# Two-layer decoder trunk: one more pair of the second MLP in seven block products, nine landing tiles and four small ones

## The chip, the cores and the metric

The kernel runs on one NeuronCore of one Trainium2 chip. The metric is the device time of one execution in microseconds (us), lower is better; a time given for a kernel is the median of its runs. The core's engines work side by side, each through its own queue in order: PE (TensorE, matmuls), DVE (VectorE), ACT (ScalarE), POOL (GpSimd) and SP (SyncE, which here issues most of the DMAs).

## What is computed

The reference is a trunk of two layers on 256 tokens of width 1024, all in fp32:

```python
for i in range(DEPTH):                     # 2
    mix = moba_attention(h, ...) if i % 2 == 0 else dilated_attention(h, ...)
    h = layer_norm(ALPHA * h + mix, ln_mix_g[i], ln_mix_b[i])
    h = layer_norm(ALPHA * h + sq_relu_mlp(h, mlp_w_in[i], mlp_w_out[i]),
                   ln_mlp_g[i], ln_mlp_b[i])

def sq_relu_mlp(x, w_in, w_out):           # 1024 -> 4096 -> 1024
    return jnp.square(jax.nn.relu(x @ w_in)) @ w_out
```

With 256 tokens the first layer's attention is plain causal attention in 16 heads of 64. The second layer's is dilated attention in 12 heads. The change touches the second layer's MLP alone, the last part of the program, and mostly its product with w_out: 256 tokens by 4096 by 1024.

## The kernel before

Every fp32 product is made of three products of fp32r parts. A tile is split into a rounded part hi and a rest lo (`split`, L414): ACT copies the tile to hi (L416), DVE subtracts hi from it and so makes lo (L421). PE then adds hi·hi, hi·lo and lo·hi in one bank of its accumulator memory (`mm`, L426). One such product of 128 tokens, 128 inputs and 512 outputs is three matmuls of 128x512.

The weights come in fp32 by DMA from SP into landing tiles of 128x1024 (tag raw, NRAW = 8 of them, L62). They are split there into tiles whi (9) and wlo (10).

The product with w_out is cut into 16 pairs, 0 to f. A pair is 256 of the 4096 inputs, two tiles of 128. The letters in `STEPS` (L41 to L44) say how each pair is computed, and in which order. There are two ways:

- **as rows** (letter O, `do_out`, L1298): two weight tiles of 1024 columns are loaded and split (`load_w`, L431), and for each of the two tiles, token halves (m = 0 and 1) and column halves there is one product: eight products, 24 matmuls.
- **as a block product** (letter S, `do_duo`, L1313): the two tiles, two token halves and two column halves form a product of 2x2 blocks, which is made of seven block products (Strassen's scheme in Winograd's form), 21 matmuls (`mm_duo`, L736). It needs sums of blocks on both sides. On the activations' side `duo_sums` (L640) makes four sums on DVE; where both pairs of a chunk are block products (kinds "SS", L660) the fourth sum covers 256 columns, where only one is, 128. On the weights' side `load_left` (L688) loads the first half x of the pair, splits 512 columns of it (tag sc1) and then adds the next columns to it: an accumulating DMA from POOL in two halves (`add_by_dma`, L679, L683). `load_right` (L701) loads the second half y, splits it (1024 columns), splits the summed x (1024), adds x into y and y's halves with two DVE adds of 512 (L782), and splits y again (1024).

Four of the seven products are gathered in four banks of their own (p1, p5, p6, p7) over all pairs. The step z (`combine_alpha`, L1356) combines them on DVE and adds the result to the token rows `tok` together with ALPHA times the residual. What comes after z in the list is "late": its items are rows (`tail`), and `out_and_ln` (L1187) multiplies them for the first 128 tokens, then for the second. The first 128 tokens are then normalised by `ln_half` (L1150), the second by `ln_last` (L1119). The latter divides its 1024 columns into 512 in one bank (left), 256 in another (right), and 256 in an extra bank (`tp`), which comes last.

A LayerNorm on DVE is: BN_STATS over pieces of the row (L1129, L1132, L1159), BN_AGGR (L1099), the power −1/2 on POOL (L1101 or L1106), subtract the mean and scale by g (`stt`, L789, operands mv,g), scale by rstd and add b (L789, operands rstd,b), and store (`store`, L1115).

The results of relu and square pass through tiles ta of 128x512 (`relu_sq`, L1225; NTA = 6, L61), as do the temporary of `combine_alpha` and some of the attention's tiles. `BEHIND_X` (L218) names the pairs whose second split goes into one of the two tiles xs, which hold the MLP's input until its first product is done, instead of whi and wlo.

The order of all work is written out: each operation is recorded by a planner (`Plan`), and the table `ORDER` (L231 on, a list of differences) gives the sequence in which they are issued. Each engine's queue is the part of that sequence that belongs to it, and an instruction that waits holds up those behind it on its engine. `out_and_ln`, `ln_last` and the others fix what depends on what, not the order.

Of the kernel before, what the change touches and what calls it, by code (L numbers as in the profile page):

```python
# [38 lines left out]
HEAD1 = '00'  # L39
STEPS = (  # L40
    "f1 f2 f3:S2:S3 f4:S4:S5 f5:S6:S7 f6:S8:S9 f7:Sa:Sb Sc Sd m g Se z Of O0 O1",  # L41
    "f1 f2 f3:S2:S3 f4:S4:S5 f5:S6:S7 f6:S8:S9 f7:Sa:Sb Sc Sd g Se z Of O0 O1",
)
SQUARES = ("ADDDAAAA", "ADDDAAAA")  # L44
AHEAD_SUM = (True, False)
# [12 lines left out]

OTAGS = {"o": "acc", "p": "tp", "t": "tp"}
HOMES = (("ta", "ta"), ("pt0", "pt1"), ("pt0", "pt1"), ("sc0", "pt1"))  # L60
NTA = 6  # L61
NRAW = 8  # L62
NFIRST = 6
PER = 1024 // (NFIRST * P)

# [4 lines left out]

STAGE_HOME = (("raw", NRAW),) * 4 + (("g", 1), ("b", 1)) + (("tok", 2),) * 2

# [67 lines left out]
class Plan:  # L140
# [74 lines left out]
LEAD = 3  # L215
ADDS = ({2: 0, 3: 0, 5: 0, 7: 0, 9: 0, 11: 0, 13: 0},) * 2
LATE_ENG = "ACT"
BEHIND_X = {12: 0, 13: 1, 14: 0}  # L218
PREPARED = ((("v", 2), ("v", 2), ("g", 1), ("b", 1)), (("ahi", 3), ("alo", 3), ("ahi", 3), ("alo", 3)))
PLANES = ((("sc0", 4), ("sc0", 4)), (("pt0", 2), ("pt1", 2)))  # L220

# [126 lines left out]
)  # L348


# [5 lines left out]
def tile_trunk(  # L356
# [37 lines left out]
    def mk(shape, dt, tag, bufs, space=None):  # L394
        uid[0] += 1
        return plan.buf(Bufs(space or sb, bufs), shape, dt, tag, bufs, f"{tag}_{uid[0]}")
# [7 lines left out]
    def act(n, aps=0, sbuf=False):  # L404
        return n / 1200 + (0.093 if sbuf else 0.055) + 0.093 * aps
# [25 lines left out]
    def load_w(src, n=1024):  # L431
        w = W()
        w.raw = mk([P, 1024], F32, "raw", NRAW)
        w.hi = mk([P, 1024], F32R, "whi", NSLOT["whi"])
# [253 lines left out]
    def load_left(pair, adds):  # L688

        x = mk([P, 1024], F32, "raw", NRAW)  # L690
        hi, lo = [mk([P, 512], F32R, "sc1", 4) for _ in range(2)]
# [9 lines left out]
    def load_right(pair, left, adds, home=None):  # L701

        x, xk, hi, lo = left
        y = mk([P, 1024], F32, "raw", NRAW)
        yk = [(y, 0), (y, 1)]
# [86 lines left out]
    def rotate(xy, ropet):  # L792
# [10 lines left out]
        for half, ps in enumerate(xy):  # L803
            ps = ps()
            b, a = mk([P, 512], F32, "ta", NTA), mk([P, 512], F32, "ta", NTA)
            src = ps
# [168 lines left out]
    def copy_out(n, ps, tag):  # L975
        t = mk([P, 512], F32, tag, NTA if tag == "ta" else 2)
        op("ACT", act(n), lambda: nc.scalar.activation(t.t[:, :n], ps.t[:, :n], AF.Copy), [ps], [t])
        return t
# [16 lines left out]
    def home(tag):  # L995
        return mk([P, 512], F32, tag, {"ta": NTA, "sc0": 4}.get(tag, 2))

# [227 lines left out]
    def relu_sq(ps, eng):  # L1225
        r = mk([P, 512], F32, "ta", NTA)
        op("ACT", act(512), lambda: nc.scalar.activation(r.t, ps.t, AF.Relu), [ps], [r])  # L1227
        if eng == "A":
            op("ACT", act(512, 0, True), lambda: nc.scalar.activation(r.t, r.t, AF.Square), [r], [r])
        else:  # L1230
            tt(512, lambda: r.t, lambda: r.t, lambda: r.t, ALU.mult, [r], [r])
        return r
# [11 lines left out]
    class Mlp:  # L1244
# [17 lines left out]
        def rest(self, between):  # L1262
# [50 lines left out]
            def do_duo(p):  # L1313
# [6 lines left out]
                for k, n in enumerate(duos[at:]):  # L1320
                    if n not in lefts and k <= LEAD:
                        begin(n)
                    if n == p:
                        w1, w2, w3, w4, w5, w6, w7 = load_right(wout[i][p], lefts[p], ADDS[i].get(p, 1), BEHIND_X.get(p))
                a11, a12, a22, s1, s2, s3, s4 = do_pair(p)
# [16 lines left out]
            def combine():  # L1342
                p1, p5, p6, p7 = prods
                z0, z1 = xtok
                t = mk([P, 512], F32, "ta", NTA)
                w = lambda x: (lambda: x.t)
# [9 lines left out]
            def combine_alpha():  # L1356
                p1, p5, p6, p7 = prods
                z0, z1 = xtok
                t = mk([P, 512], F32, "ta", NTA)
                w = lambda x: (lambda: x.t)  # L1360
# [354 lines left out]
```

## Time and profile before

| | us |
|---|---|
| three runs | 536.36, 536.97, 537.08 |
| median | 536.97 |
| the profiled execution, own time | 535.33 |
| its span in the profile | 533.5 |
| around the span | 1.83 |

| engine | busy us | share of the span |
|---|---|---|
| PE, matmuls | 525.0 | 98% |
| PEld, weight loads beside them | 435.6 | 82% |
| DVE | 502.3 | 94% |
| ACT | 426.9 | 80% |
| POOL | 28.8 | 5% |

The profile is one execution. Times are counted from the start of the span. In a timeline each line gives the start, the duration, engine, line of the kernel, operation, output <- inputs by the program's names, shapes and how many equal instructions were joined; in brackets stand the idle time just before it and what ended that. Durations on DVE and ACT overlap the next instruction's start a little, and matmuls overlap much, so the price of one in a row is the distance of two starts. In the windows the number in brackets behind a busy time is the number of instructions, and PEclk is the clock that TensorE was granted, 1.00 being full speed. The LayerNorm behind the second attention stands at 361 us; everything behind that is the second MLP, and the last matmul ends at 526.6.

### The profile page before, as it was taken

The numbers are of one execution on the slowest core, as the hardware profiler recorded it, in microseconds if no ns is written. First come the engines' busy times: TensorE is split into PE (matmuls) and PEld (weight loads), VectorE is DVE, ScalarE is ACT, GpSimd is POOL, SyncE is SP. The second block draws the span as 40 slices with busy tenths as digits, with TensorE's granted clock in tenths as the row PEclk, the third lists the DMA queues.
The fourth block names the chain that finished last, engine by engine and source line by source line (L and its number), as shares of the span: only waits on it lengthen the run. The fifth ranks groups of instructions, "written<-read, shape, count | busy, mean of one in ns | idle before, by whom it ended". The sixth has DMA issues, their size and how long they took to land. (4 is left out here: it accounts for less than half of the span.)

```text
span 533.5 us, 8128 instructions
## 1 busy us (share of the span) xinstructions
PE 525.0 (98%) x2867; PEld 435.6 (82%) x2868; DVE 502.3 (94%) x801; ACT 426.9 (80%) x608; POOL 28.8 (5%) x39
## 2 busy tenths in 40 slices
PE   9999999999999999999999999999999999999994
PEld 7988888788888888887878888888888887888784
DVE  6899996998999999999999999989889999999997
ACT  6589999548999998998645579846899998999740
POOL 0000000000010111011010000001001110110101
PEclk9999999999999999999999999999999999999998
DMA  8995788539899989989965748555888898999822
GB/s 332 390 406 146 173 288 217 198 112 242 301 211 248 260 226 313 247 197 233 349 242 191 266 169 194 173 187 127 268 237 218 226 303 219 279 273 201 250 82 79
DMA packets 79721, 123.68 MB, mean 232 GB/s; under 512 B 51264, under 2 KB 52160, under 8 KB 79680
## 3 DMA queue, kind: packets, MB, share of 16 engines
q1 hardware_dynamic: 76320, 113.26, 69.3%
q0 software_dynamic: 1920, 6.29, 7.6%
q10 hardware_dynamic: 1440, 3.61, 2.1%
q8 instruction: 22, 0.36, 0.3%
q14 instruction: 19, 0.16, 0.1%
HBM read 110.30 MB, written 1.05 MB: 209 GB/s over the span
## 5 line engine op out<-in xcount | busy, mean ns | idle before, releaser
L421 DVE TENSOR_TENSOR wlo<-raw,whi 128x1024 fp32r<-128x1024 f32 (+2 forms) x206 | 240.6, 1192 | 10.6 <-ACT whi L416 10.0
L416 ACT ACTIVATE whi<-raw 128x1024 fp32r<-128x1024 f32 (+2 forms) x204 | 206.1, 1038 | 38.2 <-PE acc L426 10.3
L426 PE MATMUL acc<-whi,xs 128*128 128x512 f32 (+1 forms) x400 | 118.7, 383 | 0.3 <-ACT ta L1227 0.2
L426 PEld LDWEIGHTS acc<-whi,xs 128*128 128x128 f32 x400 | 73.5, 188 | 15.6 <-ACT ta L1227 0.8
L426 PE MATMUL tp<-whi,xs 128*128 128x512 f32 x240 | 70.8, 393 | 0.0
L426 PE MATMUL acc<-xs,whi 128*128 128x512 f32 (+1 forms) x272 | 67.1, 358 | 0.0
L426 PE MATMUL acc<-wlo,xs 128*128 128x512 f32 (+1 forms) x200 | 66.0, 381 | 0.0
L426 PE MATMUL acc<-whi,ahi 128*128 128x512 f32 (+1 forms) x146 | 57.2, 392 | 0.0
L426 PE MATMUL acc<-wlo,ahi 128*128 128x512 f32 (+1 forms) x146 | 56.4, 386 | 0.0
L426 PE MATMUL acc<-whi,alo 128*128 128x512 f32 (+1 forms) x146 | 55.7, 386 | 0.0
L426 PEld LDWEIGHTS tp<-whi,xs 128*128 128x128 f32 x240 | 44.6, 188 | 9.0
L426 PEld LDWEIGHTS acc<-xs,whi 128*128 128x128 f32 x272 | 45.1, 190 | 6.3 <-ACT xs L416 0.7
L426 PEld LDWEIGHTS acc<-wlo,xs 128*128 128x128 f32 x200 | 37.6, 188 | 7.3 <-issue 0.2
L426 PE MATMUL acc<-xs,wlo 128*128 128x256 f32 x224 | 41.9, 281 | 0.0
L426 PE MATMUL tp<-wlo,xs 128*128 128x512 f32 x120 | 41.9, 389 | 0.0
L426 PEld LDWEIGHTS acc<-xs,wlo 128*128 128x128 f32 x224 | 35.5, 190 | 2.9
L683 POOL DMA_DIRECT2D raw<-in_wout_dram x24 | 20.0, 962 | 243.9 <-DVE sc L421 149.9
L426 PEld LDWEIGHTS acc<-whi,alo 128*128 128x128 f32 x146 | 27.4, 188 | 5.8 <-DVE alo L421 0.2
L426 PEld LDWEIGHTS acc<-whi,ahi 128*128 128x128 f32 x146 | 27.5, 188 | 5.5 <-issue 0.3
L426 PEld LDWEIGHTS acc<-wlo,ahi 128*128 128x128 f32 x146 | 27.5, 188 | 5.4 <-DVE wlo L421 0.3
L782 DVE TENSOR_TENSOR raw<-raw,raw 128x512 f32<-128x512 f32 x40 | 27.2, 683 | 0.1
L782 DVE TENSOR_TENSOR raw<-raw 128x512 f32<-128x512 f32 x40 | 27.2, 682 | 0.0
(176 smaller groups left out, 861.3 us busy)
## 6 DMA issues: line engine op xcount, KB each, us to landing
raw<-in_win_dram SPq DMA_DIRECT2D x64, 512.0 KB, 5.1
raw<-in_wout_dram SPq DMA_DIRECT2D x64, 512.0 KB, 5.5
raw<-in_wqk_dram SPq DMA_DIRECT2D x22, 512.0 KB, 7.9
raw<-in_wo_dram SPq DMA_DIRECT2D x14, 512.0 KB, 5.0
raw<-in_wout_dram POOLq DMA_DIRECT2D x24, 256.0 KB, 6.9
raw<-in_wv_dram SPq DMA_DIRECT2D x8, 512.0 KB, 5.5
raw<-in_wv1a_dram SPq DMA_DIRECT2D x4, 512.0 KB, 6.6
tok<-in_xw_dram SPq DMA_DIRECT2D x2, 512.0 KB, 7.0
```

The costliest lines, as they stand in the source:

```text
L416: a = op("ACT", act(n, sbuf=sbuf), lambda: nc.scalar.activation(hi(), src(), AF.Copy), r, whi)
L421: lambda: nc.vector.tensor_tensor(lo(), src(), f32(hi()), op=ALU.subtract), list(r) + list(whi), wlo,
L426: nc.tensor.matmul(out_ap, lhsT, rhs, start=start, stop=stop)
L683: "POOL", ADD_ISSUE, lambda rows=rows: nc.gpsimd.dma_start(dst()[rows], src()[rows], accum_op=ALU.add),
L782: op("DVE", dve(n) + extra, lambda: nc.vector.tensor_tensor(out_ap(), a(), b(), op=alu), r, w)
```

## The change

Pair f of the second MLP becomes a block product and moves ahead of the combination z: fourteen of the sixteen pairs instead of thirteen. The late items are then those of pairs 0 and 1, four instead of six. Two of the six ta tiles (128x512) go, and a ninth landing tile (128x1024) takes their room. Pair f's second split goes into xs1 (`BEHIND_X`, 15:1). `ORDER` is new from the second layer's attention on; all queues are as before up to about DVE's instruction 518 of 787, and the lines of the new kernel are one higher, since the table is one line longer.

```diff
@@ -39,7 +39,7 @@
 STEPS = (
     "f1 f2 f3:S2:S3 f4:S4:S5 f5:S6:S7 f6:S8:S9 f7:Sa:Sb Sc Sd m g Se z Of O0 O1",
-    "f1 f2 f3:S2:S3 f4:S4:S5 f5:S6:S7 f6:S8:S9 f7:Sa:Sb Sc Sd g Se z Of O0 O1",
+    "f1 f2 f3:S2:S3 f4:S4:S5 f5:S6:S7 f6:S8:S9 f7:Sa:Sb Sc Sd g Se Sf z O0 O1",
 )
@@ -58,8 +58,8 @@
-NTA = 6
-NRAW = 8
+NTA = 4
+NRAW = 9
@@ -215,7 +215,7 @@
-BEHIND_X = {12: 0, 13: 1, 14: 0}
+BEHIND_X = {12: 0, 13: 1, 14: 0, 15: 1}
@@ -307,44 +307,45 @@
-    141, -140, 141, -140, 213, -72, 14, 1, -14, -141, 91, -90, 109, -108, 41, 79, 34, -64, -48, 113, -154, 112, 43,
+    141, -140, 141, -140, 213, -72, 14, 1, -14, -141, 142, -141, 1, 89, -88, 40, 100, -166, 133, 46, -64, 65, -42,
...
```

The end of DVE's queue, before. tok_278 are the rows of the first 128 tokens, tok_324 those of the second, acc_ and tp_ are banks, tp_5497 the extra one:

```order
L789 SCALAR_TENSOR_TENSOR tok_278<-tok_278,rstd_5587,b_5565 128x512
L789 SCALAR_TENSOR_TENSOR tok_324<-tok_324,acc_4523 128x512
L789 SCALAR_TENSOR_TENSOR tok_278<-tok_278,rstd_5587,b_5565 128x512
L1129 BN_STATS bst_5592<-tok_324 128x6
L1112 TENSOR_SCALAR bst_5592<-bst_5592 128x1
L1129 BN_STATS bst_5592<-tok_324 128x6
L1132 BN_STATS bst_5592<-tp_5497 128x6
L1099 BN_AGGR mv_5616<-bst_5592 128x2
L789 SCALAR_TENSOR_TENSOR tok_324<-tp_5497,mv_5616,g_5510 128x256
L789 SCALAR_TENSOR_TENSOR tok_324<-tok_324,mv_5616,g_5510 128x768
L789 SCALAR_TENSOR_TENSOR tok_324<-tok_324,rstd_5620,b_5565 128x128
L789 SCALAR_TENSOR_TENSOR tok_324<-tok_324,rstd_5620,b_5565 128x384 x2
```

The end of DVE's queue with the change (tp_5545 is the extra bank):

```order
L790 SCALAR_TENSOR_TENSOR tok_278<-tok_278,mv_5588,g_5533 128x512
L790 SCALAR_TENSOR_TENSOR tok_324<-tok_324,acc_4644 128x512
L1133 BN_STATS bst_5590<-tp_5545 128x6
L1130 BN_STATS bst_5590<-tok_324 128x6 x2
L790 SCALAR_TENSOR_TENSOR tok_278<-tok_278,rstd_5596,b_5512 128x512
L1100 BN_AGGR mv_5616<-bst_5590 128x2
L790 SCALAR_TENSOR_TENSOR tok_278<-tok_278,rstd_5596,b_5512 128x512
L790 SCALAR_TENSOR_TENSOR tok_324<-tp_5545,mv_5616,g_5533 128x256
L790 SCALAR_TENSOR_TENSOR tok_324<-tok_324,mv_5616,g_5533 128x768
L790 SCALAR_TENSOR_TENSOR tok_324<-tok_324,rstd_5619,b_5512 128x128
L790 SCALAR_TENSOR_TENSOR tok_324<-tok_324,rstd_5619,b_5512 128x384 x2
```

The two scalings of tok_278 by rstd and b and the BN_STATS of tok_324's left 512 columns stood ahead of the BN_STATS of the extra bank and stand behind it now; the first scaling stands ahead of BN_AGGR, the second behind it.

DVE's queue where the weights of the last pairs are split, before. whi_5443 and whi_5372 are pair f's, as rows; raw_5280 and raw_5292 are the halves y and x of pair e:

```order
L421 TENSOR_TENSOR alo_5411<-qlo_5333,ahi_5397 128x1024
L421 TENSOR_TENSOR alo_5413<-m_1132_5347,ahi_5380 128x768
L782 TENSOR_TENSOR raw_5280<-raw_5280,raw_5292 128x512
L421 TENSOR_TENSOR wlo_5432<-raw_5345,whi_5372 128x1024
L782 TENSOR_TENSOR raw_5280<-raw_5280 128x512
L421 TENSOR_TENSOR xs_1_74<-raw_5292,xs_1_74 128x1024
L789 SCALAR_TENSOR_TENSOR tok_278<-tok_278,tp_4449 128x512
L421 TENSOR_TENSOR wlo_5467<-raw_5280,whi_5441 128x1024
L421 TENSOR_TENSOR wlo_5471<-raw_5395,whi_5443 128x1024
L421 TENSOR_TENSOR wlo_5473<-raw_5390,whi_5423 128x1024
```

The same place with the change; raw_5315 and raw_5303 are the halves x and y of pair f, qlo_5320 and m_1132_5361 the activations and their sums of the last chunk:

```order
L422 TENSOR_TENSOR sc_1144_5385<-raw_5315,sc_1143_5359 128x512
L783 TENSOR_TENSOR qlo_5320<-qlo_5320 128x2x128
L783 TENSOR_TENSOR m_1132_5361<-qlo_5320,m_1132_5361 128x2x128
L422 TENSOR_TENSOR wlo_5414<-raw_5303,whi_5349 128x1024
L783 TENSOR_TENSOR raw_5220<-raw_5220,raw_5246 128x512
L422 TENSOR_TENSOR alo_5433<-qlo_5320,ahi_5390 128x1024
L783 TENSOR_TENSOR raw_5220<-raw_5220 128x512
L422 TENSOR_TENSOR wlo_5437<-raw_5370,whi_5423 128x1024
L422 TENSOR_TENSOR alo_5444<-m_1132_5361,ahi_5416 128x768
L422 TENSOR_TENSOR xs_1_74<-raw_5246,xs_1_74 128x1024
L422 TENSOR_TENSOR wlo_5450<-raw_5220,whi_5439 128x1024
L783 TENSOR_TENSOR raw_5303<-raw_5303,raw_5315 128x512
```

Pair f's first lo part (sc_1144_5385) now opens the stretch, and the add that reads the sum made by DMA (raw_5303<-raw_5303,raw_5315) closes it; between them stand the last chunk's block sums and splits, pair e's adds and the splits of e and of pair 0.

75 rows, old and new, of the table ORDER are left out of this document.

## The prediction

> **What bounds the kernel now.** I read the page's busy shares first, then windows from the second attention's LayerNorm on, behind which the program changes; then DVE's waits there, and last the timelines of DVE and PE at the end.
>
> ```profile
> PE 525.0 (98%) x2867; PEld 435.6 (82%) x2868; DVE 502.3 (94%) x801; ACT 426.9 (80%) x608; POOL 28.8 (5%) x39
> ```
>
> ```profile
> core 0: us, PE busy (x) PEld busy (x) DVE busy (x) ACT busy (x) POOL busy (x), PEclk, DMA share, GB/s
> 361.20:392.00 30.80, 30.80 (x142) 25.47 (x141) 26.25 (x33) 23.48 (x29) 1.40 (x1) 1.00 0.80 209
> 392.00:500.00 108.00, 107.66 (x473) 88.35 (x472) 107.26 (x139) 102.23 (x121) 9.94 (x12) 1.00 0.93 244
> 500.00:526.80 26.80, 26.61 (x134) 22.14 (x132) 26.77 (x40) 10.67 (x13) 0.56 (x1) 1.00 0.33 121
> 526.80:533.50 6.70, 0.00 (x0) 0.00 (x0) 3.60 (x8) 0.40 (x1) 1.08 (x2) 0.76 0.33 119
> ```
>
> PE and DVE are both full. PE is so in every stretch, at a granted clock of 1.00. DVE has room in the first stretch alone: 30.80 − 26.25 = 4.55 us, then 0.74 and 0.03, together 5.3 us. ACT has 5.8 us free in the long stretch and most of the third, so it isn't the bound. What DVE waited for most in the first stretch (us in total, times, longest):
>
> ```profile
> DVE wlo L421 <- ACT whi L416: 3.5, 4, 1.4
> ```
>
> So DVE's room lies early, in front of ACT's copies of weights. The end of the kernel, on DVE and then PE's last matmul:
>
> ```profile
> 525.41 0.75 DVE L789 SCALAR_TENSOR_TENSOR tok<-tok,rstd,b 128x512 f32<-128x512 f32 x1
> 526.07 0.42 DVE L1129 BATCH_NORM_STATS2 bst<-tok 128x6 f32<-128x256 f32 x1
> 526.40 0.14 DVE L1112 TENSOR_SCALAR bst<-bst 128x1 f32<-128x1 f32 x1
> 526.46 0.42 DVE L1129 BATCH_NORM_STATS2 bst<-tok 128x6 f32<-128x256 f32 x1
> 526.79 0.42 DVE L1132 BATCH_NORM_STATS2 bst<-tp 128x6 f32<-128x256 f32 x1
> 527.24 0.26 DVE L1099 BATCH_NORM_AGGREGATE mv<-bst 128x2 f32<-128x24 f32 x1
> 527.61 0.48 DVE L789 SCALAR_TENSOR_TENSOR tok<-tp,mv,g 128x256 f32<-128x256 f32 x1
> 528.01 1.01 DVE L789 SCALAR_TENSOR_TENSOR tok<-tok,mv,g 128x768 f32<-128x768 f32 x1
> 528.94 1.60 DVE L789 SCALAR_TENSOR_TENSOR tok<-tok,rstd,b 128x128 f32<-128x128 f32 x3
> ```
>
> ```profile
> 526.21 0.28 PE L426 MATMUL tp<-wlo,ahi 128*128 128x256 f32 x1
> 526.33 0.28 PE L426 MATMUL tp<-whi,alo 128*128 128x256 f32 x1
> ```
>
> PE ends at 526.61, and 0.18 us later DVE reads the last bank; it has no gap ahead of that, so both arrive together. From there to DVE's end, 528.94 + 1.60 = 530.54, stand 3.75 us of DVE, and 3.0 us of stores behind it. The end is set by whichever of PE and DVE comes last, and by what stands in DVE's queue behind the last bank.
>
> **PE: less work.** Pair f as rows is two items of twelve 512-wide matmuls (some of them cut in 256); as seven blocks it is 21.
>
> ```profile
> 504.77 0.39 PE L426 MATMUL acc<-whi,ahi 128*128 128x512 f32 x1
> 505.00 0.39 PE L426 MATMUL acc<-wlo,ahi 128*128 128x512 f32 x1
> ```
>
> Starts are 0.23 us apart (0.2275 over longer runs of them), so PE loses 3 × 0.2275 = 0.68 us. What else PE could win are its stalls after 361 us, of which there are two:
>
> ```profile
> 447.75 0.39 PE L426 MATMUL acc<-whi,alo 128*128 128x512 f32 x1
> 448.32 0.73 PE L426 MATMUL acc<-whi,xs 128*128 128x512 f32 x2 [0.18 <-ACT ta L1227]
> ```
>
> ```profile
> 498.88 0.39 PE L426 MATMUL tp<-whi,g 128*128 128x512 f32 x1
> 499.43 0.50 PE L426 MATMUL tp<-wlo,g 128*128 128x512 f32 x1 [0.16 <-DVE wlo L421]
> ```
>
> They are 0.57 − 0.23 = 0.34 and 0.55 − 0.23 = 0.32, with small ones behind them at most 0.9 us. I leave them in, since the second is a wait for DVE, which gets more to do.
>
> **DVE: more work.** As rows the pair costs two lo parts of 1024 columns; as blocks one of 512 and three of 1024, and two adds of 512 (one of 1024 more goes to DMA, in two issues of POOL). The block sum of the activations (`duo_sums`, now kinds "SS") grows from 128 to 256 columns. Prices are from start to next start:
>
> ```profile
> 496.43 0.42 DVE L782 TENSOR_TENSOR m<-qlo 128x256 f32<-128x256 f32 x1
> 496.76 0.68 DVE L782 TENSOR_TENSOR raw<-raw 128x512 f32<-128x512 f32 x1
> 497.37 0.87 DVE L782 TENSOR_TENSOR m<-qlo,m 128x256 f32<-128x256 f32 x2
> ...
> 499.29 0.28 DVE L782 TENSOR_TENSOR qlo<-qlo 128x128 f32<-128x128 f32 x1
> 499.49 1.22 DVE L421 TENSOR_TENSOR wlo<-raw,whi 128x1024 fp32r<-128x1024 f32 x1
> 500.63 1.22 DVE L421 TENSOR_TENSOR xs<-raw,xs 128x1024 fp32r<-128x1024 f32 x1
> ...
> 502.90 0.95 DVE L421 TENSOR_TENSOR alo<-m,ahi 128x768 fp32r<-128x768 f32 x1
> 503.77 0.69 DVE L782 TENSOR_TENSOR raw<-raw,raw 128x512 f32<-128x512 f32 x1
> ```
>
> So 1.14 for 1024 (499.49 to 500.63), 0.60 for 512 (496.76 to 497.37; a lo part or an add), 0.87 for 768, and 0.33 − 0.20 = 0.13 for the wider sum: 1.14 + 3 × 0.60 + 0.13 = 3.07, with more digits (1.136, 0.602) 3.08 us. [...]
>
> How much of 3.08 goes into DVE's early room? That room is a wait on PE: a weight's hi copy needs a slot that PE gives back.
>
> ```profile
> 356.98 0.63 PE L924 MATMUL tp<-ident,tok 128*128 128x128 f32 x4
> ```
>
> ```profile
> 391.19 1.23 DVE L421 TENSOR_TENSOR wlo<-raw,whi 128x1024 fp32r<-128x1024 f32 x1 [1.06 <-ACT whi L416]
> ```
>
> For the wait at 391.19 I count in the program's order from the LayerNorm. DVE's queue from 361.20 (13 × 1.136 + 12 × 0.602 + 2.74 for small ones) would be there at 385.93, so 5.26 us of waits lie in it by then. PE's 133 matmuls from 356.98, with 16 small ones at 0.11, free the slot at 389.0; DVE starts 2.2 later. In the new order the same sort of wait comes later. Its DVE queue (22 × 1.136 + 21 × 0.602 + 8 × 0.336 + 0.87 + 2.74) reaches it at 405.13, PE's 214 matmuls free the slot at 407.43, and with 1.4 to 2.2 us for ACT the room used by then is 3.7 to 4.5 us. The next such wait (DVE 434.2, PE 436.55) gives the same. So waits of 5.26 become 3.7 to 4.5: 0.8 to 1.6 us are absorbed, and up to 0.5 of the 0.74 later. DVE comes 3.08 − 0.8 to 3.08 − 2.1, that is 1.0 to 2.3 us later to its end; I take the middle, +1.65.
>
> **The tail's order.** Behind the statistics of the last bank stand, in the new order, two more BN_STATS of 256 and two scalings of the first rows' halves (r,b, 128x512), which stood ahead of it. If DVE is in time these wait for PE's end: 2 × 0.33 (526.07 to 526.40) + 2 × 0.66 (525.41 to 526.07) − 0.1 (the gap behind 527.24 is filled) = 1.89 us. PE's end is 0.68 earlier, so this way gives +1.2. If DVE is late, the order costs nothing of its own, since all of it must be done anyway. It can be late without PE: from the last lo part on, DVE's queue up to that bank holds 10.0 us (eleven steps of 512 at 0.60 and nine smaller or scaled ones, 3.4), PE's some 9.1 (26 matmuls at 0.2275, 25 of 256 at 0.12, and the start). The two don't add: the end is the later of +1.2 and +1.65.
>
> **ACT, POOL, SP and the buffers.**
>
> ```profile
> 389.17 2.00 ACT L416 ACTIVATE whi<-raw 128x1024 fp32r<-128x1024 f32 x2
> ```
>
> ```profile
> 492.35 0.68 DVE L421 TENSOR_TENSOR sc<-raw,sc 128x512 fp32r<-128x512 f32 x1
> ```
>
> ```profile
> 493.44 1.65 POOL L683 DMA_DIRECT2D raw<-in_wout_dram  x2 [13.08 <-DVE sc L421]
> ```
>
> ```profile
> raw<-in_wout_dram POOLq DMA_DIRECT2D x12, 256.0 KB, 7.2
> ```
>
> ACT gets one copy of 1024 and one of 512, at most 2 × 1.00 us, beside its 5.8 free ones: nothing; without that cover it would be those 2 us. POOL issues two more adding DMAs (0.83 each). From f's first lo part to the sum's landing I count 1.1 + 0.8 + 7.2 = 9.1 us by the last pair's rows; DVE has between it and the add that reads the sum 9.0 us of queue. A tie: 0 to +0.8, and I take 0. The loads through SP lead their readers by over 7 us, and a ninth landing tile only adds to it. Four small ta tiles for six: up to the second attention, where the order is the same, no wait of PE moves; behind it the one row that names ta is the stall of 0.34, so 0 to +0.35, and I take 0. BEHIND_X puts f's second weights into xs1, free by then: nothing.
>
> **Sum.** +1.65, rounded to +1.6: the profiled execution of 535.33 (a span of 533.5, where the last window ends, and 1.83 around it) becomes 536.9. The median of the runs shown is 1.64 above that execution, so I forecast 536.97 + 1.6 = 538.6.
>
> **Rivals.**
> (a) Not slower. DVE's waits all melt (5.3 are more than 3.08), it is in time, PE's end decides, and PE's stalls go as well, since the ninth landing tile lets ACT and DVE run ahead: −0.68 − 0.9 + 1.89 = +0.3, and with 0.5 of smaller stalls elsewhere −0.2. It decides when DVE reads the last bank under 0.3 us after PE's end. For it: the room exists. Against: the room is early and tied to PE, and from 392 on DVE shows 0.77 us of idle in 134.8.
> (b) DVE absorbs nothing, since the waits on ACT copies stay as they are: +3.08, less 0.5 at the best, with the late sum 3.6 at the worst; around +2.9, or 539.9. [...]
> (c) The change doesn't do what it says, or fewer ta tiles stall some place that I haven't seen: anything from −1.5 to +4.
>
> **How the numbers follow.** A measurement here tells 0.2%, or 1.07 us, from no change. The forecast case (+0.9 to +2.3) has 0.55, (a) (−0.2 to +0.9) 0.20, (b) (+2.1 to +3.6) 0.20, (c) 0.05. Slower by over 1.07: nearly all of the forecast case (0.50), (b), and a little of (c): 0.71. Faster by that much: (c) and what the bounds of (a) miss, 0.05. Within: 0.24. For 8 in 10 I leave out the bottom of (a), the top of (b) and (c): +0.2 to +3.1, that is 537.2 to 540.1.
>
> **What would show it.** Right: DVE's end at 531.5 to 533 (before 530.54), PE's last matmul up to 1.1 us before the statistics of the last bank, and 5 to 6 us of DVE, not 3.75, from these on; DVE idle in 361 to 392 and just behind it down by about 1 us, and nearly none from 410 on; PE stalls named DVE in the last 100 us. For (a): PE's last matmul at 525.9 or before. For (b): DVE's idle as large as before, and PE waits of 2 us for wlo. Wrong altogether: DVE's chain behind PE's end under 4 us, or PE's end over 1 us earlier than 525.9.

## The result, and the profile after

| | kernel before | changed kernel | ratio (95% interval) |
|---|---|---|---|
| first series, 6 and 6 runs, us | 536.66 | 540.06 (538.88 to 542.30) | 1.0077 (1.0060 to 1.0093) |
| again, beside the first experiments, us | 536.01 | 541.33 (540.06 to 542.24) | 1.0090 (1.0070 to 1.0111) |

By the ratios, which are worked out from all runs and not from the two medians, the change costs 0.77 to 0.90%, that is 4.1 to 4.8 us, where I forecast 1.6 (the medians alone differ by 3.4 and 5.3 us). The sign was right; the size lies above the range of 0.2 to 3.1 us (537.2 to 540.1 about a median of 536.97). The first median, 540.06, still falls inside 537.2 to 540.1, but the kernel before was 0.3 us faster in that series than the median from which I forecast.

The profiled execution of the changed kernel took 542.30 us, the slowest of its six, with a span of 540.5. Its LayerNorm behind the second attention stands at 361.94, 0.8 us later than before. DVE is 1.6 us behind already at 50 us, where the queues are the same, and in a second profile of the changed kernel (e_again below) the LayerNorm stands at 361.39; so I count this part as scatter. The windows of the changed kernel, cut as those of before:

```profile
core 0: us, PE busy (x) PEld busy (x) DVE busy (x) ACT busy (x) POOL busy (x), PEclk, DMA share, GB/s
361.20:392.00 30.80, 30.80 (x142) 25.52 (x141) 28.70 (x37) 23.23 (x28) 0.92 (x1) 1.00 0.65 196
392.00:500.00 108.00, 106.36 (x468) 87.47 (x467) 105.15 (x132) 100.54 (x118) 9.93 (x12) 1.00 0.94 241
500.00:526.80 26.80, 24.76 (x104) 19.23 (x103) 23.80 (x32) 14.55 (x17) 1.65 (x2) 0.94 0.54 138
```

In the first stretch DVE does 2.45 us more than before (28.70 against 26.25): the early room is used. Behind it both engines, which were full, have gaps: DVE 2.85 and 3.00 us, PE 1.64 and 2.04, and PE's clock falls to 0.94 in the last. What DVE waited for from 361 us to the end, and PE in the whole span (us in total, times, longest; the longest entries):

```profile
DVE wlo L422 <- ACT whi L417: 2.8, 5, 1.2
DVE raw L783 <- DMA raw<-in_wout_dram: 2.4, 2, 2.1
DVE sc L422 <- ACT sc L417: 0.9, 1, 0.9
```

```profile
PE tp L427 <- DVE xs L422: 1.8, 2, 1.2
PE acc L427 <- ACT ta L1228: 1.1, 1, 1.1
...
PE tp L427 <- DVE wlo L422: 0.7, 1, 0.7
```

Behind 361 us a wait of DVE for a DMA is new. It lies at pair f's sum. DVE there, the POOL issues of that sum, and PE a little later:

```profile
509.91 1.23 DVE L422 TENSOR_TENSOR wlo<-raw,whi 128x1024 fp32r<-128x1024 f32 x1
513.28 0.69 DVE L783 TENSOR_TENSOR raw<-raw,raw 128x512 f32<-128x512 f32 x1 [2.14 <-DMA raw<-in_wout_dram]
```

```profile
503.12 1.65 POOL L684 DMA_DIRECT2D raw<-in_wout_dram  x2 [6.77 <-DVE qlo L783]
```

```profile
515.86 0.39 PE L427 MATMUL tp<-xs,ahi 128*128 128x512 f32 x1
517.50 0.50 PE L427 MATMUL tp<-xs,ahi 128*128 128x512 f32 x1 [1.25 <-DVE xs L422]
517.84 0.40 PE L427 MATMUL tp<-xs,alo 128*128 128x512 f32 x1
518.07 0.39 PE L427 MATMUL tp<-whi,ahi 128*128 128x512 f32 x1
519.19 0.50 PE L427 MATMUL tp<-wlo,ahi 128*128 128x512 f32 x1 [0.73 <-DVE wlo L422]
```

DVE reads the sum 10.2 us after the first issue (503.12 to 513.28). DVE stands 2.14 us, and ACT, which copies the same sum to hi, 3.5 us; f's second weight pair (xs) and three tail weights behind it on ACT come late, and PE loses 1.41 us (517.50 − 515.86 − 0.23) and 0.89. The end, on DVE and PE:

```profile
531.22 0.68 DVE L790 SCALAR_TENSOR_TENSOR tok<-tok,acc 128x512 f32<-128x512 f32 x1
532.11 0.43 DVE L1133 BATCH_NORM_STATS2 bst<-tp 128x6 f32<-128x256 f32 x1 [0.21 <-PE tp L427]
532.46 0.74 DVE L1130 BATCH_NORM_STATS2 bst<-tok 128x6 f32<-128x256 f32 x2
533.11 0.74 DVE L790 SCALAR_TENSOR_TENSOR tok<-tok,rstd,b 128x512 f32<-128x512 f32 x1
...
535.85 1.41 DVE L790 SCALAR_TENSOR_TENSOR tok<-tok,rstd,b 128x128 f32<-128x128 f32 x3
```

```profile
531.79 0.28 PE L427 MATMUL tp<-whi,alo 128*128 128x256 f32 x1
```

Behind the last bank's statistics stand 537.26 − 532.11 = 5.15 us of DVE, as forecast (5 to 6), and PE and DVE arrive there together; but both come 5.3 to 5.5 us later than before.

### The profile page after: what moved, and what is told of

Read it like the earlier page. It is cut to its first block, busy times and chain, and to the rows that moved or that the text cites. A ratio compares the mean times of both kernels' runs of the same rounds, so it can differ in the third digit from the quotient of the medians.

```text
span 540.5 us, 8132 instructions
## 1 busy us (share of the span) xinstructions
PE 526.6 (97%) x2858; PEld 435.6 (81%) x2859; DVE 505.2 (93%) x805; ACT 429.0 (79%) x610; POOL 31.1 (6%) x41
## 4 chain that ended last, share of the span: by engine, by line
PE 80%; DVE 9%; DMA 4%; issue 3%; ACT 2%; POOL 0%; POOLq 0%; ACTq 0%; DVEq 0%
PE acc L427 51%; PE tp L427 27%; DVE wlo L422 4%; DMA raw<-in_wout_dram 3%; DVE tok L790 1%; PE tp L925 1%; DVE raw L783 1%; ACT whi L417 1%; DMA raw<-in_xw_dram 1%; DVE alo L422 0%; DVE sc L422 0%; DVE tok L783 0%; DVE m L783 0%; DVE bst L1160 0%; DVE b L422 0%
## 5 line engine op out<-in xcount | busy, mean ns | idle before, releaser
L427 PE MATMUL acc<-whi,ahi 128*128 128x512 f32 (+1 forms) x141 | 56.0, 397 | 0.0
L427 PE MATMUL acc<-wlo,ahi 128*128 128x512 f32 (+1 forms) x141 | 55.1, 391 | 0.1
L427 PE MATMUL acc<-whi,alo 128*128 128x512 f32 (+1 forms) x141 | 54.3, 390 | 0.0
L684 POOL DMA_DIRECT2D raw<-in_wout_dram x26 | 21.7, 961 | 253.0 <-DVE sc L422 195.0
L783 DVE TENSOR_TENSOR raw<-raw,raw 128x512 f32<-128x512 f32 x41 | 28.3, 695 | 2.5 <-DMA raw<-in_wout_dram 2.4
L783 DVE TENSOR_TENSOR raw<-raw 128x512 f32<-128x512 f32 x41 | 28.3, 695 | 0.0
```

Of the source, the lines that this page charges most:

```text
L427: nc.tensor.matmul(out_ap, lhsT, rhs, start=start, stop=stop)
L684: "POOL", ADD_ISSUE, lambda rows=rows: nc.gpsimd.dma_start(dst()[rows], src()[rows], accum_op=ALU.add),
L783: op("DVE", dve(n) + extra, lambda: nc.vector.tensor_tensor(out_ap(), a(), b(), op=alu), r, w)
```

## The experiments

Two theories stood after this. **L:** data land late, and the waits for them, not the work, are what the forecast missed. **W:** DVE's 3.08 us of new work is paid in full (the prediction's rival b). Times are medians; each is compared with the kernel before, run beside it on the same chip.

**e_again**, the changed kernel once more.

> The changed kernel once more, unaltered, for a second profile. Theory L (late sum): pair f's sum by DMA lands after DVE and ACT want it, and the wait for it, the PE stalls behind it and the half clock behind these make up most of what the forecast missed; then the wait of DVE for that DMA is here again, 1 to 3 us, and the time is 3.4 to 4.1 us above the kernel before. Rival W (work): DVE's 3.08 us of new work is paid in full and the wait for the sum is an accident of one execution; then the time is the same 3.4 to 4.1 us above, with no wait of DVE for a DMA, and with DVE's idle after 361 us under 5.3 us.

541.33 us against 536.01, 4.8 us by the ratio and 5.3 by the medians, so more than the 3.4 to 4.1 that both theories gave. DVE's wait is there again, at the same place, so it isn't an accident of one execution:

```profile
DVE raw L783 <- DMA raw<-in_wout_dram: 2.5, 1, 2.5
```

**e_add**, pair f's sum by DVE (ORDER goes with it).

```diff
-ADDS = ({2: 0, 3: 0, 5: 0, 7: 0, 9: 0, 11: 0, 13: 0},) * 2
+ADDS = ({2: 0, 3: 0, 5: 0, 7: 0, 9: 0, 11: 0, 13: 0}, {2: 0, 3: 0, 5: 0, 7: 0, 9: 0, 11: 0, 13: 0, 15: 0})
```

> Pair f's sum is made by two DVE adds of 512 columns instead of the accumulating DMA: DVE gets 2 x 0.60 = 1.20 us more to do, and there is no landing to wait for. Theory L: 2.0 to 3.5 us faster than the changed kernel (waits of 2.1 on DVE and 2.0 on PE, and 1.3 of half clock go, 1.2 comes). Rival W: 1.2 us slower than the changed kernel.

540.71 us against 536.01, ratio 1.0074 (1.0051 to 1.0096): 0.6 below e_again, inside the spread of both, and neither theory's number. Its profile says why it doesn't decide: the wait for f's sum is gone, but another landing was worse in that execution, a weight of the first product, which ACT and then PE waited for:

```profile
466.55 1.06 ACT L417 ACTIVATE whi<-raw 128x1024 fp32r<-128x1024 f32 x1 [2.85 <-DMA raw<-in_win_dram]
```

```profile
471.71 0.73 PE L427 MATMUL acc<-whi,xs 128*128 128x512 f32 x2 [2.65 <-ACT ta L1228]
```

In e_again the same ACT copy waits 1.46 us for its DMA. In the changed kernel's first profile it waits 1.76 us and starts at 465.84; the view names PE there, but the data, issued at 458.58, land 7.2 us later, at 465.8. That widened L: there is a second late landing, and it is not the sum.

**e_early**, pair f's sum earlier. The edit is in ORDER; as a diff of the queues, in names of the changed kernel (raw_5315 is f's first half, raw_5303 its second):

```diff
 SP   -load raw_5303   -load raw_5315
 SP   +load raw_5315   +load raw_5303
 DVE   xs_1_74<-raw_5118,xs_1_74 128x1024
 DVE  +sc_1144<-raw_5315,sc_1143 128x512
 DVE   wlo_5351<-raw_5225,whi_5342 128x1024
 DVE   m_1132<-qlo_5320 128x2x128
 DVE   xs_2_75<-raw_5095,xs_2_75 128x1024
 DVE   m_1132<-qlo_5320,m_1132 128x2x128
 DVE  -sc_1144<-raw_5315,sc_1143 128x512
```

(The hi copy on ACT and the two POOL issues move with it.)

> Pair f's first half is loaded ahead of its second, and its hi copy, its first lo part and the two POOL issues of the sum move up by about 3.5 us in their queues; no work is added. Theory L: 2.0 to 4.0 us faster than the changed kernel, and no wait of DVE for that DMA. Rival W: within 0.5 us of the changed kernel.

538.35 us against 536.01, ratio 1.0039 (1.0022 to 1.0055): 3.0 us below e_again by the medians, 2.7 by the ratios, with the same work. The wait is gone:

```profile
498.74 0.81 POOL L684 DMA_DIRECT2D raw<-in_wout_dram  x1 [3.83 <-DVE sc L422]
```

```profile
508.48 1.22 DVE L422 TENSOR_TENSOR wlo<-raw,whi 128x1024 fp32r<-128x1024 f32 x1
509.61 0.68 DVE L783 TENSOR_TENSOR raw<-raw,raw 128x512 f32<-128x512 f32 x1
```

The adding DMAs land no faster here (from issue to landing the median is 7.4 us and the longest 9.5, in the changed kernel 7.3 and 9.9); the sum only has more time. About 0.4 us of the gain lies ahead of it: PE's wait for ta near 470 us is 0.4 us, and 0.8 in e_again. L holds for the sum; W does not.

**e_tail**, the changed kernel with the old end of DVE's queue.

```diff
+L790 SCALAR_TENSOR_TENSOR tok_278<-tok_278,rstd_5596,b_5512 128x512
 L790 SCALAR_TENSOR_TENSOR tok_324<-tok_324,acc_4644 128x512
+L790 SCALAR_TENSOR_TENSOR tok_278<-tok_278,rstd_5596,b_5512 128x512
+L1130 BN_STATS bst_5590<-tok_324 128x6 x2
 L1133 BN_STATS bst_5590<-tp_5545 128x6
-L1130 BN_STATS bst_5590<-tok_324 128x6 x2
-L790 SCALAR_TENSOR_TENSOR tok_278<-tok_278,rstd_5596,b_5512 128x512
 L1100 BN_AGGR mv_5616<-bst_5590 128x2
-L790 SCALAR_TENSOR_TENSOR tok_278<-tok_278,rstd_5596,b_5512 128x512
```

> The changed kernel with the end of DVE's queue as before the change: both scalings of the first rows by rstd and b, and the statistics of the second rows' left columns, ahead of the statistics of the extra bank. The prediction's claim (the end is the later of two ways, and DVE is late): 0 to 0.4 us faster than the changed kernel. Rival O (the order's 1.89 us stand in full behind PE's end): 1.9 us faster, with 3.2 to 3.8 us of DVE behind the statistics of the extra bank and no wait for DVE ahead of it.

541.38 us against 536.01, ratio 1.0084 (1.0064 to 1.0105): e_again's time within the scatter. The claim holds: where DVE isn't early, the old order of its last steps brings nothing that these runs can tell.

**e_el**, early sum and two exchanges of loads on SP. The second late landing is a matter of landing tiles: in e_early the last of two loads is issued at 455.49 + 2.67 − 0.33 = 457.8. No tile is free earlier: in the program this load takes the tile that the DVE step ending at 457.80 reads last, and the other eight are held longer. ACT is ready for the data 5.9 us after the issue, at 463.70 (the three rows are SP's, DVE's and ACT's):

```profile
455.49 2.67 SPq L413 DMA_DIRECT2D raw<-in_win_dram  x2
```

```profile
456.58 1.22 DVE L422 TENSOR_TENSOR wlo<-raw,whi 128x1024 fp32r<-128x1024 f32 x1
```

```profile
464.76 1.06 ACT L417 ACTIVATE whi<-raw 128x1024 fp32r<-128x1024 f32 x1 [1.06 <-DMA raw<-in_win_dram]
```

The exchange loads those two ahead of two that are wanted later (and does the same for one pair of w_out loads, whose reader waited 1.67 us at 488 in the changed kernel):

```diff
-L413 DMA raw_4988<-in_wout_dram 128x1024
-L413 DMA raw_5006<-in_wout_dram 128x1024
-L413 DMA raw_5011<-in_win_dram 128x1024
-L413 DMA raw_5020<-in_win_dram 128x1024
+L413 DMA raw_4988<-in_win_dram 128x1024
+L413 DMA raw_5006<-in_win_dram 128x1024
+L413 DMA raw_5011<-in_wout_dram 128x1024
+L413 DMA raw_5020<-in_wout_dram 128x1024
```

> Pair f's sum early as in e_early, and the loads of weights on SP in another order at two places, so that the two weights that ACT waited for (at 465 and 488 us) take landing tiles that come free earlier; no work is added. Theory L, widened (late landings, of the sum and of two weights, are what the forecast missed): DVE's waits of 0.9 to 2.6 us there go, PE's stall of 0.4 to 2.7 us before ACT's ta goes, and the time is 0.8 to 2.0 us below e_early, so 0.3 to 1.5 us above the kernel before. Rival W (DVE's added work is paid in full, loads don't matter once the sum is early): within 0.4 us of e_early, 2.3 us above the kernel before.

536.05 us against 535.88, ratio 1.0003 (0.9993 to 1.0013): level with the kernel before, with all of the change's work in it, and a little below the range that L gave. Its windows, and its end on DVE and PE:

```profile
361.20:392.00 30.80, 30.80 (x141) 25.55 (x140) 28.68 (x37) 23.09 (x28) 0.92 (x1) 1.00 0.65 206
392.00:500.00 108.00, 108.00 (x478) 89.41 (x478) 107.75 (x138) 103.26 (x121) 11.59 (x14) 1.00 0.95 245
500.00:526.80 26.80, 25.48 (x123) 20.75 (x121) 26.33 (x41) 11.96 (x14) 0.87 (x1) 1.00 0.41 112
```

```profile
526.10 0.42 DVE L1133 BATCH_NORM_STATS2 bst<-tp 128x6 f32<-128x256 f32 x1
...
529.84 1.40 DVE L790 SCALAR_TENSOR_TENSOR tok<-tok,rstd,b 128x128 f32<-128x128 f32 x3
```

```profile
525.21 0.28 PE L427 MATMUL tp<-whi,alo 128*128 128x256 f32 x1
```

PE has no gap from 392 to 500, DVE 0.25 us, and 0.47 behind that; PE ends at 525.49 and DVE, at 526.10, is late by 0.6. Whether an earlier sum or other loads would also help the kernel before wasn't run; the prediction puts its PE stalls behind 361 us at 0.9 us at most.

**e_elt**, e_el with the old end of DVE's queue, edited as in e_tail.

> As e_el, with the end of DVE's queue as before the change (scalings and left statistics ahead of the statistics of the extra bank). Claim of the prediction: the tail's order counts only if DVE is in time. If e_el leaves DVE late (statistics of the extra bank wait for nothing), this is within 0.3 us of e_el; if DVE is in time there (it waits for PE ahead of them), this is 1.0 to 1.9 us faster than e_el.

536.42 us against 535.88, ratio 1.0009 (1.0000 to 1.0018): 0.4 us above e_el, a little over the 0.3 expected for a late DVE, and far from the gain of 1.0 to 1.9 for one in time.

**e_loads**, the two exchanges without the early sum.

> The changed kernel with the two exchanges of weight loads on SP alone; pair f's sum stays late. Theory L (late landings add up): DVE's waits of 0.9 to 2.6 us for ACT at 465 and 493 go, the wait for f's sum stays; 1.4 to 2.5 us below the changed kernel, so 2.5 to 3.9 above the kernel before. Rival S (the late sum hides the two other waits, as DVE waits for the sum anyway): within 0.5 us of the changed kernel.

538.80 us against 536.22, ratio 1.0049 (1.0037 to 1.0061), so 2.6 us above the kernel before, where the changed kernel stands 4.1 to 4.8 above. The wait for the sum is still there (2.2 us). The two repairs add up, by the ratios: the loads bring 2.2 us without the early sum (e_again to e_loads) and 1.9 with it (e_early to e_el), the early sum 2.7 without the exchanges (e_again to e_early) and 2.5 with them (e_loads to e_el). Each of these is uncertain by 1 us or so, and the two exchanges were not run one by one.

**e_dup**, the kernel before with 3.4 us more on DVE.

```diff
-            lambda: nc.vector.tensor_tensor(lo(), src(), f32(hi()), op=ALU.subtract), list(r) + list(whi), wlo,
+            lambda: [nc.vector.tensor_tensor(lo(), src(), f32(hi()), op=ALU.subtract) for _ in range(times)], list(r) + list(whi), wlo,
...
+                    item = (get, load_w(wout[i][p][:, k * 1024 : k * 1024 + 1024], times=2 if i == 1 and (p == 15 or p == 0 and k == 0) else 1), nkt - 1 if final else 0, nkt)
```

> The kernel before, with three lo parts of 1024 columns made twice on DVE (both of pair f, one of pair 0), 3 x 1.14 = 3.4 us more of DVE work near the end and nothing else. DVE full to its end (the prediction's reading of the windows): 2.9 to 3.4 us slower than the kernel before. Rival P (PE holds the end and DVE has a lead to lose): at most 2 us slower.

539.76 us against 535.88, ratio 1.0074 (1.0057 to 1.0090), 3.1 to 4.8 us, with its middle above the 2.9 to 3.4 expected: in that order, near the end, DVE's work is paid in full.

**e_buf**, the buffers alone.

```diff
-NTA = 6
-NRAW = 8
+NTA = 4
+NRAW = 9
```

> The kernel before with four small ta tiles instead of six and nine landing tiles instead of eight, its order unchanged. The prediction priced this at nothing: within 0.4 us of the kernel before. Rival B (fewer ta tiles stall the queues): 0.8 to 2 us slower.

535.92 us against 535.88, ratio 0.9997 (0.9987 to 1.0007): nothing, in the old order.

**e_pool1 and e_pool2**, e_el with less of the tail on DVE (e_pool2 without the "and n == 0", its second add behind the second power on POOL; ORDER goes with both).

```diff
-            stt(512, 1, lambda c=c: z.t[:, c], lambda c=c: z.t[:, c], lambda: rs.t[:, 1:2], lambda c=c: b.t[:, c],
-                ALU.mult, ALU.add, [(z, n), (rs, 1), b], [(z, n)])
+            if last and n == 0:
+                op("ACT", act(512, 1, True), lambda c=c: nc.scalar.activation(z.t[:, c], z.t[:, c], AF.Copy, scale=rs.t[:, 1:2]),
+                   [(z, n), (rs, 1)], [(z, n)])
+                op("POOL", 1.7, lambda c=c: nc.gpsimd.tensor_tensor(z.t[:, c], z.t[:, c], b.t[:, c], op=ALU.add), [(z, n), b], [(z, n)])
+            else:
+                stt(512, 1, lambda c=c: z.t[:, c], lambda c=c: z.t[:, c], lambda: rs.t[:, 1:2], lambda c=c: b.t[:, c],
+                    ALU.mult, ALU.add, [(z, n), (rs, 1), b], [(z, n)])
```

> As e_el, with the last scaling of one half of the first rows (r,b, 128x512, 0.66 us of DVE) made by ACT (scale by rstd) and POOL (add b) instead of DVE. If DVE's work ends the kernel, as in e_el's profile, 0.4 to 0.7 us below e_el, so 0.2 to 0.5 us below the kernel before. Rival: POOL's add of 512 columns delays the power of the second LayerNorm behind it on POOL, or DVE beside it: within 0.3 us of e_el, or above it.

> As e_pool1, with both halves: 1.32 us off DVE; the second half's add stands behind the second power on POOL. If DVE's work ends the kernel: 0.8 to 1.3 us below e_el, which beats the kernel before by 0.6 to 1.1 us. Rival: the second add on POOL (a 128-column one took 1.06 us at e_el's end) and the last small add behind it end the kernel: 0.5 to 2 us above e_el.

e_pool1: 535.38 us against 536.22, ratio 0.9983 (0.9970 to 0.9997). It is the one version here that beats both kernels, by 0.03 to 0.30% over the one before, just clear of no change; its one profile is of its slowest execution and doesn't show the gain. e_pool2: 536.10 against 536.22, ratio 1.0007 (0.9992 to 1.0021), no gain, and neither of the two numbers expected. In its profile the second add runs on POOL beside DVE's last scalings, and these take 2.61 us where e_el's take 1.40:

```profile
528.93 1.90 POOL L1170 TENSOR_TENSOR tok<-tok,b 128x512 f32<-128x512 f32 x1
```

```profile
529.63 2.61 DVE L790 SCALAR_TENSOR_TENSOR tok<-tok,rstd,b 128x128 f32<-128x128 f32 x3
```

## Why the prediction was wrong, point by point

- **Pair f's sum ("a tie: 0 to +0.8, and I take 0").** This step failed first. The 9.0 us of DVE's queue were right (502.03, f's first lo part, to 511.05, when DVE is ready to add). The other side, 9.1 us, was made with the median landing of 7.2, and the sum came at 513.28, after 11.25. In the trace of before, ACT waited already for pair e's sum, which came 9.4 us after its first lo part (492.35 to 501.71):

```profile
501.71 1.06 ACT L416 ACTIVATE xs<-raw 128x1024 fp32r<-128x1024 f32 x1 [0.48 <-DMA raw<-in_wout_dram]
```

  That trace held also the spread in which a tie must be judged, and that of after confirms it (the POOL issues of 380 to 530 us, first of before, then of after):

```profile
DMA to landing us min/median/max: 4.1/7.2/9.3
```

```profile
DMA to landing us min/median/max: 3.8/7.3/9.9
```

  With 9.3 the upper end would have been about 2 us, the wait that was measured. And I priced DVE's wait alone: ACT waits for the same sum with three weights behind it, and PE stalls. The step, taken at 0, is worth 2.5 to 3.0 us (e_early, and e_loads to e_el).

- **"The loads through SP lead their readers by over 7 us, and a ninth landing tile only adds to it."** This step failed too, and its premise didn't hold in the trace of before, where ACT waited for a load of SP:

```profile
445.26 1.06 ACT L416 ACTIVATE whi<-raw 128x1024 fp32r<-128x1024 f32 x1 [1.46 <-DMA raw<-in_wout_dram]
```

  In the new order all nine landing tiles are held when the w_in load's turn comes. It goes out when the first of them comes free, and leads its reader by 5.9 us in e_early and 5.5 in the changed kernel. The step, taken at nothing, is worth about 2 us (both exchanges together).

- **DVE's work: "0.8 to 1.6 us are absorbed, and up to 0.5 later", so +1.65.** The size was off the other way. In e_el 2.4 us go into the first stretch alone (28.68 against 26.25) and 0.5 into the second (107.75 against 107.26); in the third DVE does 0.44 less by 526.8 (26.33 against 26.77). So its idle time from 361.2 to 526.8 fell from 5.3 to 2.8 us: 2.5 of 3.08 were absorbed, where I took 1.4. I had priced the room by one wait on PE, at the point where the old order met it; the new order meets it at another. So rival (b) does not give the result: e_el carries the whole work at +0.03%. It fits e_dup, where the work is added behind the early room.

- **The tail's order.** The chain behind the last bank is 5.15 us (forecast: 3.75 + 1.89 = 5.64 at most). That the two ways don't add was right: the old order in its place brings no gain, late landings or not (e_tail, e_elt).

- **PE's 0.68 us** are in e_el's profile: PE ends at 525.49, 1.1 us earlier than before, though its second MLP began 0.7 us later. That is 1.8 us, more than 0.68; the rest, 1.1, is near the 0.9 of stalls that I had left in. **The ta tiles and landing tiles** at nothing were right in the old order (e_buf).

- **Rival (a)**, "the ninth landing tile lets ACT and DVE run ahead", is about what e_el is: its sum of +0.3 us stands beside +0.2 measured. But it needed the loads in another order and the sum earlier, DVE still comes 0.6 us after PE there, and whether the ninth tile has a part in it wasn't run.

The forecast's +1.6 was thus the sum of a term that was too high and two that were taken at nothing. That the sign came out right was luck: the work that gave it costs +0.2 us in e_el, no more than the scatter, and the loss came from the two others. What stays open is why the changed kernel stands 4.1 us above in one series and 4.8 in the other; the two intervals overlap, and the late landings scatter (ACT's wait for the w_in weight is 1.1 to 2.9 us in the five profiles that have the same loads up to there).

## What to carry to other kernels

Where two engines are full, ask of every new transfer how long before its reader it is issued, and compare that with the longest landing in the trace (9.3 us before the change) and not with the median (7.2): here a tie by the median was a wait of 2.14 us. Count with it everyone who reads the same data, and what stands behind them on their queues. Ask also when a landing tile comes free. Where all are held, a load goes out when the next one is released, and the order of the loads decides which weight gets it; here that order was worth about 2 us.

## What the runs showed of the hardware

PE's granted clock fell to 0.56 behind short stalls. Behind the gaps of 1.41 and 0.89 us of the changed kernel, matmuls of 512 columns start 0.43 us apart from 520 to 523 us; the windows around it are these:

```profile
517.00:519.50 2.50, 1.27 (x4) 0.78 (x5) 2.03 (x3) 2.50 (x3) 0.00 (x0) 1.00 0.81 305
519.50:523.00 3.50, 3.50 (x10) 2.69 (x9) 3.50 (x5) 0.80 (x2) 0.00 (x0) 0.56 0.22 82
```

That makes 10 matmuls in 3.5 us instead of 15, about 1.2 us of loss (3.5 − 10 × 0.2275). In e_tail, with the same two stalls (waits of 1.4 and 0.7 us), matmuls of 512 columns start 0.43 us apart too, from 519.56 to 522.12, and the granted clock is 0.94 over 500 to 526.8 us, as in the changed kernel; in e_again, with them too (waits of 1.4 and 0.7), the clock stayed at 1.00:

```profile
519.50:523.00 3.50, 3.50 (x17) 2.51 (x16) 3.50 (x7) 0.03 (x1) 0.00 (x0) 1.00 0.06 23
```

So the clock behind the same two stalls differs from one execution to the next: 0.56 in the changed kernel's, 1.00 in e_again's, with the same program. No run here shows what decides it.

The second surprise is the row pair of e_pool2 above: DVE's scalings take 2.61 instead of 1.40 us beside an add on POOL. They start at 529.63, and the add runs from 528.93 to 530.83. The scaling of 768 columns ahead of them, which started before the add (528.70), takes 1.01 us as in e_el. This is one execution, and no run here shows what held the scalings.
